# A hybrid decoder trunk on one core: the place of the down projection's weight sums, and the order of the last quarter's output

## The chip, the core and the metric

The kernel runs on 1 core of one Trainium2 chip. Time is the device time of one execution in microseconds (us), 1373.87 us as the median of three runs (1373.46 to 1376.73). The engines are named as the profile names them: PE (TensorE matmul) and PEld (its weight loads), DVE (VectorE), ACT (ScalarE), POOL (GpSimd), SP (SyncE, which issues every DMA of this kernel, one after the other). Each engine works through its own program in order; semaphores make it wait for another engine or for a DMA.

## The reference

One layer with three sub-layers on x (1024 tokens, width 1024). Each is normalised before and after, and added to the residual stream:

```python
def rmsnorm(x, g):
    xf = x * lax.rsqrt(jnp.mean(x * x, axis=-1, keepdims=True) + RMS_EPS)
    return xf * g

h = rmsnorm(x, g_mix_pre)                       # 1. token mixing
s_in, s_gate, g_u, g_vv = split(h @ w_in)
y_ssm  = gelu(s5_ssm(s_in, ...)) * sigmoid(s_gate)
y_gmlp = chunked_spatial_gate(g_u, g_vv, ...)
x = x + rmsnorm(concat([y_ssm, y_gmlp]) @ w_out, g_mix_post)
h = rmsnorm(x, g_x_pre)                         # 2. cross-attention, 4 heads, 256 memory tokens
x = x + rmsnorm(memory_cross_attention(h, rmsnorm(mem, g_mem), w_q, w_k, w_v, w_o), g_x_post)
h = rmsnorm(x, g_ffn_pre)                       # 3. gated ConvFFN, d_ff = 2816
a = causal_depthwise_conv(h @ w_up, conv_w, conv_b)
val, gate = split(a)
x = x + rmsnorm((val * gelu(gate)) @ w_down, g_ffn_post)
```

All is float32.

## The kernel before

Activations lie transposed: 128 features on the partitions, tokens along the row. The 1024 tokens are two halves of 512 (`h` = 0, 1). A float32 product is done as three matmuls on a high and a low part of both operands (`mm3`, L233): ACT writes the rounded high part, DVE or POOL subtracts it from the original and gets the low part. For streamed weights that is L131 on ACT and L134 on DVE (`Stream.split_to`), for the rest L252 and L253 (`split`). Weights are loaded by SP into four `raw` buffers (L85) and split up to six tiles ahead (`W_AHEAD`).

The work goes through the sub-layers in order: `mixers` (which ends with the K and V projections of the memory), `attention`, `ffn` (up projection and convolution), `down`. In `attention`, first both halves of the mixing's output projection run ("o1", weights w_out), then for each half the query projection, scores, softmax and weighting of four heads, and the attention's output projection ("o2"). `post` finishes a sub-layer for one half: it multiplies with the post gain and the broadcast root mean square (L723 on DVE), adds the residual (L724 on POOL), accumulates squares (L709 on ACT, L710 on POOL or DVE), and prepares the next sub-layer's input (L729, L730). It is a generator that advances by a step as matmuls are recorded (`side`, `tick`).

The statistics of a normalisation are made with PE and DVE: `rms` sums squares over partitions with matmuls against ones (L278) into a PSUM bank, and `rsqrt` finds the reciprocal root in eleven tiny DVE operations (L261 to L270). `bcast` spreads it over the partitions with matmuls against the identity (L305) and copies the result to SBUF on ACT (L308). PSUM has eight banks, tagged `acc` (4), `sx` (3) and `st` (1).

The up and down projections use Strassen's form on 2 x 2 blocks. For the down projection the sums of its weights are made early: `s_sums` loads for each of 11 row blocks four tiles of w_down (L1350, `w_dk`), makes four sums on POOL (L1354) and stores them to DRAM (L1355, `sd`). That is 44 loads, 44 sums and 44 stores. Each call of `next` makes one of 22 steps, by turns loads and sums. In the kernel before, the steps are taken in the attention's two halves: 14 steps, thus 28 sums, in the first, and the other 16 sums in the second.

`down` runs three phases of 11 blocks over four banks A and four banks B, and a fourth that completes A for the second half's tokens, first for its columns 0 to 255 (a quarter of all tokens), then for 256 to 511. Beside the fourth phase the first half's output is finished by `finish`: squares, `rms`, `bcast`, then for eight tiles the multiplication (L766, DVE), the residual (L767, POOL) and the store (L769). The second half's quarters are finished by `finish_pair` (L774 and L776, on DVE or POOL). `squares` (L1515 on ACT, L1516 on DVE) accumulates their sums of squares. `TAIL_R` and `TAIL_B` say after which (column block, row block) of the last quarter the first quarter's `rms` and `bcast` are recorded.

The order within each engine's program is set by a scheduler from the recorded order and its own estimates. Only instructions given to `pin` while `self.pinned` is set keep the order in which they are written.

## Time and profile before

| | |
|---|---|
| median of three runs | 1373.87 us (1373.46 to 1376.73) |
| profiled execution | 1375.64 us |
| its span (first to last instruction) | 1373.8 us |
| mean granted TensorE clock | 0.967 |
| PE / DVE / ACT / POOL busy | 1275.9 / 1066.1 / 628.0 / 694.6 us |
| DMA moved | 233.58 MB, 170 GB/s in the mean |

A row of the profile names a line, an engine, an operation and its tiles, output first (`m<-m,rs` writes tile m from m and rs). "Idle before" is how long the engine stood still ahead of the row, and the arrow names what ended the wait. `xN` is a count. A PE matmul of 128x512 here takes 0.23 us at the full clock; the granted clock falls to 0.5 in some stretches. SPq is SP's queue, whose rows are issues of DMAs.

### The profile page before, as it was taken

To read this page: it belongs to the slowest core of one execution; us is meant where nothing else is said; L and a number is where in the kernel's file an instruction comes from. 1 tells how busy PE (TensorE), PEld (TensorE's weight loads), DVE (VectorE), ACT (ScalarE), POOL (GpSimd) and SP (SyncE) were. 2 spreads that over 40 slices of the span, in tenths; PEclk is the share of its full clock that TensorE was granted. 3 is DMA by queue.
4 is the path that set the end of the run, shared out by engine and by line. 5 is a ranking of instruction groups with operands and counts; after the bars stand their busy time and mean duration, and the time that the engine had idled before them with its cause. 6 is when DMAs were issued, how large, how long until landed. Compare 5 with 4: busy or idle time off the path is not lost. (4 is left out here: it accounts for less than half of the span.)

```text
span 1373.8 us, 19246 instructions
## 1 busy us (share of the span) xinstructions
PE 1275.9 (93%) x6352; PEld 1080.4 (79%) x6352; DVE 1066.1 (78%) x1619; ACT 628.0 (46%) x1172; POOL 694.6 (51%) x532
## 2 busy tenths in 40 slices
PE   9799898779998999769999999999999999999993
PEld 7689897678886888558887878888888888788883
DVE  7968799876377757796657978888899879966576
ACT  7223331246444445345544654555555554446340
POOL 1586355834258524860343838656565227822144
PEclk9899999899998999979999999999999999999996
DMA  9654326256348844772358566545454359755123
GB/s 319 185 143 134 93 73 182 85 148 192 93 125 263 299 134 125 266 245 85 83 163 282 161 209 229 180 149 161 146 182 140 107 198 383 233 159 175 56 79 136
DMA packets 150662, 233.58 MB, mean 170 GB/s; under 512 B 33697, under 2 KB 43041, under 8 KB 150561
## 3 DMA queue, kind: packets, MB, share of 16 engines
q1 hardware_dynamic: 150560, 232.34, 53.3%
q8 instruction: 50, 0.82, 0.3%
q14 instruction: 52, 0.42, 0.1%
HBM read 174.23 MB, written 53.85 MB: 166 GB/s over the span
## 5 line engine op out<-in xcount | busy, mean ns | idle before, releaser
L233 PE MATMUL acc<-b,w 128*128 128x512 f32 x2412 | 587.9, 397 | 11.4 <-DVE b L730 4.4
L233 PEld LDWEIGHTS acc<-b,w 128*128 128x128 f32 x2412 | 457.6, 191 | 110.2 <-DVE b L730 6.5
L134 DVE TENSOR_TENSOR w<-raw,w 128x512 fp32r<-128x512 f32 x206 | 203.1, 994 | 94.2 <-PE acc L233 64.6
L233 PE MATMUL sx<-b,w 128*128 128x512 f32 x921 | 222.6, 391 | 1.7 <-ACT T L1277 1.7
L233 PEld LDWEIGHTS sx<-b,w 128*128 128x128 f32 x921 | 174.0, 189 | 38.5 <-ACT T L1277 2.1
L131 ACT CAST w<-raw 128x512 fp32r<-128x512 f32 x228 | 141.4, 622 | 125.3 <-PE acc L233 72.1
L710 POOL TENSOR_TENSOR ac<-ac,sq 128x512 f32<-128x512 f32 x52 | 78.3, 1513 | 153.2 <-ACT sq L709 152.6
L233 PE MATMUL acc<-T,w 128*128 128x512 f32 x528 | 127.0, 389 | 0.0
L233 PEld LDWEIGHTS acc<-T,w 128*128 128x128 f32 x528 | 99.1, 188 | 20.5
L253 DVE TENSOR_TENSOR w<-b,w 128x512 fp32r<-128x512 f32 x64 | 67.4, 1065 | 23.7 <-PE st L233 8.6
L1400 POOL TENSOR_TENSOR f<-f,f 128x512 f32<-128x512 f32 x33 | 55.0, 1678 | 48.1 <-DMA f<-fd 35.5
L1354 POOL TENSOR_TENSOR m<-m,m 128x512 f32<-128x512 f32 x44 | 62.8, 1432 | 31.3 <-DMA m<-in_w_dk 22.3
L724 POOL TENSOR_TENSOR m<-m,rs 128x512 f32<-128x512 f32 x32 | 49.3, 1545 | 48.6 <-DMA rs<-x1d 18.9
L233 PE MATMUL sx<-T,w 128*128 128x512 f32 x264 | 66.5, 389 | 0.0
L253 DVE TENSOR_TENSOR b<-f,b 128x512 fp32r<-128x512 f32 x53 | 54.4, 1041 | 4.3 <-ACT b L252 4.0
L233 PEld LDWEIGHTS sx<-T,w 128*128 128x128 f32 x264 | 49.6, 188 | 10.3
L709 ACT ACTIVATE sq<-m 128x512 f32<-128x512 f32 x66 | 41.3, 630 | 30.6 <-POOL m L724 13.5
L1216 POOL TENSOR_TENSOR b<-b,m 128x512 f32<-128x512 f32 x22 | 32.5, 1478 | 44.7 <-ACT m L1215 44.2
L115 POOL TENSOR_TENSOR st<-st,b 128x512 f32<-128x512 f32 x20 | 26.6, 1328 | 52.5 <-DMA st<-in_w_up 29.4
L252 ACT CAST w<-b 128x512 fp32r<-128x512 f32 x64 | 39.5, 619 | 27.3 <-PE acc L233 16.9
L233 PE MATMUL acc<-w,b 128*128 128x256 f32 x384 | 50.9, 290 | 0.0
L252 ACT CAST b<-f 128x512 fp32r<-128x512 f32 x53 | 32.7, 619 | 38.4 <-DVE w L253 34.3
(345 smaller groups left out, 2278.9 us busy)
## 6 DMA issues: line engine op xcount, KB each, us to landing
raw<-in_w_up SPq DMA_DIRECT2D x68, 256.0 KB, 3.0
f<-fd SPq DMA_DIRECT2D x55, 256.0 KB, 4.6
m<-in_w_dk SPq DMA_DIRECT2D x44, 256.0 KB, 4.7
sd<-m SPq DMA_DIRECT2D x44, 256.0 KB, 3.8
b<-sd SPq DMA_DIRECT2D x44, 256.0 KB, 4.0
b<-in_w_up SPq DMA_DIRECT2D x40, 256.0 KB, 2.8
raw<-in_w_out SPq DMA_DIRECT2D x32, 256.0 KB, 2.7
raw<-in_w_q SPq DMA_DIRECT2D x32, 256.0 KB, 3.4
```

Of the source, the lines that this page charges most:

```text
L115: g.tensor_tensor(p["S4"], p["12"], p["S2"], ALU.subtract)
L131: nc.scalar.copy(hi[:, :w], t[:, :w])
L134: e.tensor_tensor(lo[:, :w], t[:, :w], hi[:, :w], ALU.subtract)
L233: self.pin(nc.tensor.matmul(ps, lhsT=x, rhs=y, start=first and i + j == 0, stop=last and i == n - 1 and j == 2, skip_group_check=go_on))
L252: self.nc.scalar.copy(hi, src)
L253: (e or self.nc.vector).tensor_tensor(lo, src, hi, ALU.subtract)
L709: nc.scalar.activation(sq, src, AF.Square)
L710: (e or nc.gpsimd).tensor_tensor(acc, acc, sq, ALU.add)
L724: g.tensor_tensor(x, x, rs, ALU.add)
L1216: nc.gpsimd.tensor_tensor(val, val, gate, ALU.mult)
L1354: g.tensor_tensor(t[to], t[x], t[y], op)
L1400: self.nc.gpsimd.tensor_tensor(s[to], s[x], s[y], ALU.subtract)
```

## The change

The diff, without the parts that only move a line:

```diff
-TAIL_R = (1, 1)
-TAIL_B = (1, 9)
+TAIL_R = (0, 7)
+TAIL_B = (1, 3)
+JOB_AT = (8,)
...
-    def rms(self, acc, nt):
+    def rms(self, acc, nt, bank="st"):
...
-        ps = self.bank("st")
+        ps = self.bank(bank)
...
-    def bcast(self, r, nt, tag="st"):
+    def bcast(self, r, nt, tag="st", bank="st"):
...
-        ps = self.bank("st")
+        ps = self.bank(bank)
...
     def finish(self, m, acc, h, x2d):
...
-        r, bc = yield from self.stats(acc, 4)
+        r = self.rms(acc, 4)
+        yield
+        bc = self.bcast(r, 4)[0]
+        yield
         for i in range(KT):
             x = m[i]
-            v.scalar_tensor_tensor(x, x, self.gain["g_ffn_post"][:, i:i + 1], bc, ALU.mult, ALU.mult)
-            g.tensor_tensor(x, x, res[i], ALU.add)
+            self.pin(v.scalar_tensor_tensor(x, x, self.gain["g_ffn_post"][:, i:i + 1], bc, ALU.mult, ALU.mult))
+            e = v if i % 4 == 3 else g
+            self.pin(e.tensor_tensor(x, x, res[i], ALU.add))
+            nc.sync.dma_start(self.out[P * i:P * i + P, HALF * h:HALF * h + HALF], x)
             yield
-            nc.sync.dma_start(self.out[P * i:P * i + P, HALF * h:HALF * h + HALF], x)
...
+        s_job = self.s_sums()
         kv = self.side(kv_parts(), 1)
         for h in range(2):
             for b in range(8):
                 proj(lambda k, hh: self.mix[k, hh], "o1", m1, sq1, b, h, (4, 5, 6, 7, 0, 1, 2, 3))
+                if h == 0:
+                    next(s_job)
...
-        s_job = self.s_sums()
...
             if h == 0:
+                self.drain(s_job)
                 self.side(post[1])
...
-                    t[o, j] = self.slot("m")
+                    t[o, j] = self.slot("t" if k < 4 else "m")
...
+        next(job)
+        next(job)
         for k in range(11):
...
-            next(job, None)
-        self.drain(job)
+            if k in JOB_AT:
+                next(job)
         st = {}
+        self.pinned = True
         for b in range(4):
-            self.pinned = b > 0
             for k in range(11):
                 one(k, b, quarters[1])
+                if k % 2 == 0 and b < 2:
+                    next(job, None)
                 if (b, k) == TAIL_R:
-                    st["r"] = self.rms(sq[1][:, quarters[0]], 2)
+                    st["r"] = self.rms(sq[1][:, quarters[0]], 2, "sx")
                 if (b, k) == TAIL_B:
-                    bc = self.bcast(st["r"], 2)[1]
+                    bc = self.bcast(st["r"], 2, "st", "sx")[1]
```

Eight steps of `s_sums` (16 loads, 16 sums, 16 stores) are now taken in the first half of "o1", in tiles of the tag `t` (11 buffers), and the other 14 in the first half's attention as before; the second half's attention has none. In the tail, `finish` is advanced by a step after every second row block of the last quarter's first two column blocks, its multiplication reads the broadcast in PSUM, two of its eight additions go to DVE, and the order of all this is fixed. The first quarter's statistics come earlier and use a bank `sx`.

In the changed kernel all lines behind the edits have moved by 1 to 12: L85 is L86 there, L710 is L711, L724 is L725, L766 is L770, L767 is L772, L1350 is L1358, L1354 is L1362, L1355 is L1363 and L1516 is L1524.

SP's program where "o1" begins, in the kernel before (`raw<-in_w_v` are loads of the V projection's weights, `raw<-in_w_out` those of "o1"):

```order
L85 DMA raw_3482<-in_w_v 128x512
L85 DMA raw_3488<-in_w_v 128x512
L85 DMA raw_3519<-in_w_out 128x512
L85 DMA raw_3552<-in_w_out 128x512
L85 DMA raw_3560<-in_w_out 128x512
L85 DMA raw_3566<-in_w_out 128x512
L85 DMA raw_3597<-in_w_out 128x512
```

The same place in the changed kernel, from the fourth load of w_out on (`sd` are the stored sums):

```order
L86 DMA raw_3566<-in_w_out 128x512
L1363 DMA sd_0_229<-t_3691 128x512
L1363 DMA sd_0_251<-t_3689 128x512
L86 DMA raw_3597<-in_w_out 128x512
L1363 DMA sd_1_230<-t_3807 128x512
L1363 DMA sd_0_240<-t_3685 128x512
L86 DMA raw_3629<-in_w_out 128x512
L1363 DMA sd_1_252<-t_3805 128x512
L86 DMA raw_3653<-in_w_out 128x512
L1363 DMA sd_0_262<-t_3687 128x512
L1358 DMA t_3915<-in_w_dk 128x512
L86 DMA raw_3675<-in_w_out 128x512
```

Stores and loads of the sums now stand between the loads of w_out; ahead of these rows eleven loads of `in_w_dk` stand among the last four loads of w_v and the first three of w_out.

POOL's program in the second half's attention, in the kernel before (L710 accumulates squares, L1354 is a sum, L724 adds a residual):

```order
L710 TENSOR_TENSOR ac_5333<-ac_5333,sq_5748 128x512
L1354 TENSOR_TENSOR m_5907<-m_5907,m_5905 128x512
L1354 TENSOR_TENSOR m_6030<-m_6026,m_6030 128x512
L1354 TENSOR_TENSOR m_6026<-m_6032,m_6026 128x512
L1354 TENSOR_TENSOR m_6028<-m_6028,m_6026 128x512
L1354 TENSOR_TENSOR m_6169<-m_6167,m_6169 128x512
L1354 TENSOR_TENSOR m_6167<-m_6163,m_6167 128x512
L1354 TENSOR_TENSOR m_6163<-m_6169,m_6163 128x512
L1354 TENSOR_TENSOR m_6165<-m_6165,m_6163 128x512
L1354 TENSOR_TENSOR m_6302<-m_6300,m_6302 128x512
L724 TENSOR_TENSOR m_5331<-m_5331,rs_5933 128x512
L724 TENSOR_TENSOR m_5390<-m_5390,rs_5988 128x512
```

The same place in the changed kernel:

```order
L711 TENSOR_TENSOR ac_5397<-ac_5397,sq_5708 128x512
L711 TENSOR_TENSOR ac_5397<-ac_5397,sq_5750 128x512
L711 TENSOR_TENSOR ac_5397<-ac_5397,sq_5812 128x512
L725 TENSOR_TENSOR m_5395<-m_5395,rs_5989 128x512
L725 TENSOR_TENSOR m_5454<-m_5454,rs_6036 128x512
```

The residuals now follow the squares directly.

DVE's program in the tail, in the kernel before, from the last square of the first quarter to the first step of that quarter's reciprocal root (L281 reads the sums of squares from PSUM):

```order
L1516 TENSOR_TENSOR ac_11081<-ac_11081,sq_13145 128x256
L766 SCALAR_TENSOR_TENSOR m_12201<-m_12201,gains,st_12982 128x512
L766 SCALAR_TENSOR_TENSOR m_12206<-m_12206,gains,st_12982 128x512
L766 SCALAR_TENSOR_TENSOR m_12211<-m_12211,gains,st_12982 128x512
L766 SCALAR_TENSOR_TENSOR m_12216<-m_12216,gains,st_12982 128x512
L766 SCALAR_TENSOR_TENSOR m_12221<-m_12221,gains,st_12982 128x512
L766 SCALAR_TENSOR_TENSOR m_12226<-m_12226,gains,st_12982 128x512
L766 SCALAR_TENSOR_TENSOR m_12231<-m_12231,gains,st_12982 128x512
L766 SCALAR_TENSOR_TENSOR m_12236<-m_12236,gains,st_12982 128x512
L281 TENSOR_SCALAR st_x<-st 128x2
```

In the changed kernel, ahead of that root and then behind it (L1524 is a square of the last quarter, L772 an addition of `finish` that went to DVE, L779 and L781 are `finish_pair`):

```order
L770 SCALAR_TENSOR_TENSOR m_12201<-m_12201,gains,st 128x512
L770 SCALAR_TENSOR_TENSOR m_12206<-m_12206,gains,st 128x512
L770 SCALAR_TENSOR_TENSOR m_12211<-m_12211,gains,st 128x512
L282 TENSOR_SCALAR st_x<-sx 128x2
L262 TENSOR_SCALAR rs_y_13126<-st_x 128x2
```

```order
L770 SCALAR_TENSOR_TENSOR m_12216<-m_12216,gains,st 128x512
L772 TENSOR_TENSOR m_12216<-m_12216,rs_13004 128x512
L770 SCALAR_TENSOR_TENSOR m_12221<-m_12221,gains,st 128x512
L1524 TENSOR_TENSOR ac_11081<-ac_11081,sq_13153 128x256
L770 SCALAR_TENSOR_TENSOR m_12226<-m_12226,gains,st 128x512
L770 SCALAR_TENSOR_TENSOR m_12231<-m_12231,gains,st 128x512
L770 SCALAR_TENSOR_TENSOR m_12236<-m_12236,gains,st 128x512
L772 TENSOR_TENSOR m_12236<-m_12236,rs_13012 128x512
L779 TENSOR_TENSOR m_12287<-m_12287,st_13181 128x512
L781 TENSOR_TENSOR m_12287<-m_12287,b_12288 128x512
```

Three multiplications of the first half stand ahead of the quarter's root instead of eight, the other five behind it. On PE the first half's broadcast stands 11 matmuls behind its sums of squares (47 before), the quarter's sums 21 matmuls behind that, and its broadcast another 21 (24 before).

## Prediction

> **What bounds the kernel now.** I read the page first (engine totals, slices), then busy time by windows, then the waits and the timeline of the windows that stand out.
>
> ```profile
> PE 1275.9 (93%) x6352; PEld 1080.4 (79%) x6352; DVE 1066.1 (78%) x1619; ACT 628.0 (46%) x1172; POOL 694.6 (51%) x532
> ...
> PE   9799898779998999769999999999999999999993
> ```
>
> PE is busy 93% of the span, so it is the bound nearly everywhere, and a change can only win in the few slices below 9. Two of them are touched: slices 17 to 19 (about 550 to 620 us, digits 7, 6, 9) and the last one. The windows give the size (columns: window, length, then PE, PEld, DVE, ACT, POOL busy, granted clock, DMA share, GB/s):
>
> ```profile
> 325.00:365.00 40.00, 39.63 (x191) 33.58 (x192) 15.39 (x20) 19.43 (x36) 8.44 (x7) 1.00 0.47 136
> 428.00:510.00 82.00, 81.50 (x405) 68.81 (x406) 54.84 (x95) 35.72 (x79) 43.70 (x32) 0.95 0.74 244
> 548.00:620.00 72.00, 52.90 (x235) 40.97 (x234) 62.22 (x87) 28.02 (x59) 51.30 (x35) 0.88 0.75 251
> 1325.00:1374.00 49.00, 24.01 (x175) 23.09 (x173) 31.97 (x59) 7.10 (x19) 21.80 (x14) 0.76 0.32 108
> ```
>
> In the second half's attention (548 to 620) PE stands idle for 72.00 - 52.90 = 19.1 us; there DVE and POOL are the busy ones. The first half's (428 to 510) loses 0.5 us, though 28 of the 44 sums run in it. The stretch to which 16 sums move (325 to 365) has a full PE, a POOL that is 79% idle and a DVE that is 62% idle. In the last 49 us PE is idle for half the time.
>
> DVE and POOL slow each other, and only for some operands:
>
> ```profile
> L766 DVE SCALAR_TENSOR_TENSOR m<-m,gains,st x8: 746/1745/1785, 1333.3 to 1343.0; 128x512 f32<-128x512 f32 x8
> L1205 DVE SCALAR_TENSOR_TENSOR t<-acc,conv,t x6: 731/739/750, 770.6 to 824.5; 128x511 f32<-128x511 f32 x6
> 770.00:780.00 10.00, 10.00 (x46) 8.29 (x45) 9.96 (x10) 4.48 (x10) 10.00 (x8) 1.00 0.78 234
> ```
>
> (A line's durations are minimum, median, maximum in ns.) With both tensors in SBUF the operation takes 0.75 us in a gap of POOL and 1.75 us beside it. The same operation with one tensor in PSUM takes 0.73 to 0.75 us, although POOL is busy all of 770 to 780.
>
> **Part 1: sixteen sums leave the second half's attention.** What they take there, and what waits:
>
> ```profile
> PE acc L233 <- DVE b L730: 4.4, 3, 2.4
> ...
> L1354 POOL TENSOR_TENSOR m<-m,m 128x512 f32<-128x512 f32 x16 | 23.6, 1477 | 10.4 <-DMA m<-in_w_dk 9.2 <-DMA rs<-x1d 0.5 <-issue 0.2
> L269 DVE SCALAR_TENSOR_TENSOR rs_t<-rs_t,st_x 128x4 f32<-128x4 f32 x6 | 4.0, 663 | 0.2
> L723 DVE SCALAR_TENSOR_TENSOR m<-m,gains,st 128x512 f32<-128x512 f32 x8 | 9.5, 1259 | 0.0
> ...
> 569.27 1.28 POOL L1354 TENSOR_TENSOR m<-m,m 128x512 f32<-128x512 f32 x1
> 574.13 1.07 DVE L261 TENSOR_SCALAR rs_y<-st_x 128x4 int32<-128x4 int32 x1
> 582.09 0.17 DVE L739 TENSOR_SCALAR rs_y<-rs_y 128x4 f32<-128x4 f32 x1
> 583.14 0.56 ACT L1128 ACTIVATE t<-sx,mx,rs_y 128x256 f32<-128x256 f32 x1 [10.65 <-DVE mx L1124]
> 585.97 1.11 PE L233 MATMUL sx<-kv,t 128*128 128x256 f32 x4 [3.47 <-ACT t L252]
> 587.73 3.31 PE L233 MATMUL acc<-b,w 128*128 128x512 f32 x10
> 598.52 5.74 PE L233 MATMUL acc<-b,w 128*128 128x512 f32 x24
> 611.40 1.12 PE L1142 MATMUL sx<-ident,t 128*128 128x128 f32 x4 [7.15 <-ACT t L1128]
> 615.88 6.99 PE L233 MATMUL acc<-b,w 128*128 128x512 f32 x21
> ...
> 610.00:620.00 10.00, 7.26 (x19) 5.51 (x20) 8.75 (x16) 6.57 (x17) 4.02 (x3) 0.50 0.71 225
> ```
>
> The tiny steps of the reciprocal root average 0.66 us here and 0.16 us elsewhere (last fence, below); the whole root takes from 574.1 to 582.3. It holds the first maxima, so the exponentials wait 10.65 us, and PE 3.47 us for the ACT copy behind them. Then eight L723 in a row (9.5 us) stand ahead of the next maxima, and PE waits 7.15 us. After it PE runs at a granted clock of 0.50: 21 matmuls take 6.99 us where 24 take 5.74, which loses 2.0 us; the 10 at 587.73 lose 0.9 us in the same way.
>
> Without the sums, POOL has nothing left between its last squares and the first L724, so the root falls from some 8 us to some 2 (eleven steps of 0.16 and their gaps) and the 3.47 us goes: **-3.5**. The L723 go from 9.5 to 8 x 0.75 = 6.0 plus about 1 each beside two L724, and the three operations ahead of the maxima lose about 1: the stall falls from 7.15 to about 3, **-4.1**. Of the 19.1 us idle, 10.6 is named so far; 4.4 is PE's wait for L730, ahead of the half's first sum at 569.27, and stays; of the other 4.1 I take half, **-2.0**. The halved clock cost 2.9 and should mostly go with the long stalls: **-2.4**. Together **-12**. The bounds: -4 (the first stall and its clock alone) and -20 (all but the 4.4, the clock, and 2 to 3 for loads that land sooner). What is late next is DVE's own row of L723 and the adds of the same sub-layer, which is why 3 us of the second stall stay.
>
> **Part 2: they arrive in the first half's output projection.** The loads there, PE's last wait before it, PE's pace, the splits of 330 to 390, and the landing of the stores that go along:
>
> ```profile
> 321.94 67.19 SPq L85 DMA_DIRECT2D raw<-in_w_out  x31
> 325.37 4.45 PE L233 MATMUL acc<-w,m 128*128 128x256 f32 x35 [0.71 <-DVE w L134]
> 803.98 5.44 PE sx L233 x24
> L134 DVE TENSOR_TENSOR w<-raw,w 128x512 fp32r<-128x512 f32 x24 | 20.1, 845 | 34.9 <-PE acc L233 33.7 <-ACT w L131 1.1
> DMA to landing us min/median/max: 2.0/3.9/6.8
> ```
>
> POOL gets 16 x 1.3 to 1.48 = 21 to 24 us on top of 8.4 of 40: it fits. DVE's splits (L134, 0.845 us mean) may go to 1.75, sixteen of them 14 us more, on 15.4 of 40: it fits. On SP the 16 stores stand between the 4th and the 18th load of weights, each waiting for its sum. Each load feeds 12 matmuls, 5.44 / 2 = 2.72 us; those 14 feed PE for 38 us. The sums with the two K/V splits and two accumulations that stand among them take POOL about 29 us, and the last five loads wait for slots whose stores land in 3.9 us, perhaps two of them one after the other: 37 us, with some six splits in stock. So PE should not wait in the middle. At the start, where PE waited 0.71 us for a split, eleven loads are put among the last of w_v and the first of w_out: I take **+1**, from nothing to +4. These are covered by POOL's and DVE's idle time; if that cover fails, see the third rival.
>
> **Part 3: the last quarter.**
>
> ```profile
> 1325.09 0.95 PE L278 MATMUL st<-ones,ac 128*128 128x1 f32 x8
> 1328.91 0.16 DVE L270 SCALAR_TENSOR_TENSOR rs_y<-rs_t,rs_y 128x4 f32<-128x4 f32 x1
> 1333.33 11.47 DVE L766 SCALAR_TENSOR_TENSOR m<-m,gains,st 128x512 f32<-128x512 f32 x8 [1.38 <-ACT st L308]
> 1344.72 0.15 DVE L281 TENSOR_SCALAR st_x<-st 128x2 f32<-128x2 f32 x1
> 1348.55 0.16 DVE L270 SCALAR_TENSOR_TENSOR rs_y<-rs_t,rs_y 128x2 f32<-128x2 f32 x1
> 1348.86 1.19 PE L305 MATMUL st<-ident,rs_y 128*128 128x128 f32 x4 [11.94 <-DVE rs_y L270]
> 1350.49 3.91 PE L233 MATMUL acc<-f,w 128*128 128x256 f32 x18
> 1356.03 2.32 PE L233 MATMUL acc<-f,w 128*128 128x256 f32 x18
> 1360.61 0.43 DVE L1516 TENSOR_TENSOR ac<-ac,sq 128x256 f32<-128x256 f32 x1 [2.37 <-ACT sq L1515]
> ...
> L774 DVE TENSOR_TENSOR m<-m,st x5: 678/686/1774, 1352.0 to 1367.1; 128x512 f32<-128x512 f32 x5
> L774 POOL TENSOR_TENSOR m<-m,st x3: 1270/1272/1734, 1350.5 to 1365.3; 128x512 f32<-128x512 f32 x3
> L269 DVE SCALAR_TENSOR_TENSOR rs_t<-rs_t,st_x 128x4 f32<-128x4 f32 x3 | 0.5, 160 | 0.1
> ```
>
> Today eight L766 stand ahead of the quarter's reciprocal root, PE waits 11.94 us, and its next 18 matmuls take 3.91 us instead of 2.32. Now only three stand ahead of it. PE's side: 11.94 + 1.6 = 13.5 us go. New waits come. The first broadcast stands 11 matmuls (1.4 us at 2.32 / 18) behind the sums of squares instead of 47, while the root is ready 3.0 us after them: PE waits 1.6 us. The quarter's broadcast waits for its own root, 4.0 us beside POOL's adds (1344.7 to 1348.7 today), of which 21 matmuls hide 2.7: 1.3, with the trip to DVE and back about 2. PE is done 9.9 us sooner.
>
> DVE's and POOL's side ends later. From 1326.0 on: root 3.0, broadcast 1.1, 21 matmuls 2.7, sums of squares 0.6, the quarter's root 4.0: 1337.4. Behind it come five multiplies at 0.75 us, which read PSUM and pass POOL by, and seven POOL operations of 1.28 us, six DVE operations of 0.68 and three squares of 0.43 that take turns: 9.0 + 4.1 + 1.3 = 14.4 us, and about 1.5 us in which POOL waits for the multiplies. The last square is added by 1353.7, not by 1361.0, and what follows (12.8 us to the end) stays: **-7.3**. Bounds: -3, if the root takes 8 us as at 574 and the multiplies 1.75, and -9.9, PE's side alone. The ACT copy of the broadcast stays in the program and the first multiply still waits for it, so nothing is counted for it.
>
> [...]
>
> **The sum** is +1 - 12 - 7.3 = **-18.3 us**. The profiled execution took 1375.64 us (its span of 1373.8 and 1.8 around it) and would take 1357.3. The median of the runs is 1373.87, 1.8 below it, so I forecast **1355.6 us**.
>
> **The rivals.**
> - *The sums did not hold the second half; its own post-processing does.* For it: 428 to 510 carries 28 sums and PE loses 0.5 us. Against it: there the first half's post-processing was over before them, and steps of 0.66 us are seen only beside a busy POOL. Part 1 would bring -5: 1 - 5 - 7.3 gives 1362.6. Chance 0.17.
> - *The tail only changes its bound.* First half and quarter now share DVE and POOL; if the root is slowed to 8 us, part 3 is -3: 1359.9. Chance 0.13. [...]
> - *The stores hold SP (slower).* If each of the 16 stores in the output projection costs SP a sum and a landing, 1.48 + 3.9 = 5.4 us, SP needs 86 us for loads that feed 38, with 16 (six splits) in stock: PE loses 32 us, and -19.3 + 32 gives 1386.6. It decides the sign from 73 us, 4.6 per store. Against it: a store does not wait for the one before it, and 28 sums go with their stores through 428 to 510. Chance 0.05.
> - *POOL held all of it*: part 1 is -20, 1347.6. Chance 0.10.
> - *The change does not do what it says*: other waits take both gains back, 1373. Chance 0.04.
>
> **How the numbers follow.** The forecast (1350 to 1359) keeps 0.51. The range, 1347 to 1365, takes in the first, second and fourth rival and their bounds and leaves out about 2 in 10: the fifth and third rival (0.09) and the far ends of the others. About 0.3%, 4.1 us, is what a measurement can tell from no change: faster 0.91, within it 0.04, slower 0.05.
>
> **What would show it.** Part 1: between 548 and 620 of the old scale PE idle falls from 19 to 8 or 9 us, L269 there is near 0.16 us, and the clock stays at 1.00. Wrong if the waits for L1128 keep their 7 us. Part 2: PE stays above 39 of 40 us in the output projection; wrong if PE waits for L134 or SP's loads of w_out stretch. Part 3: no wait of PE above 4 us after the sums of squares, L770 at 0.75 us, and 1325 to the end shorter by 7. What would make the forecast wrong is above all a new wait of PE in the first half, which no row of this profile shows.

## The result, and the profile after the change

| | before | after |
|---|---|---|
| median of the runs compared | 1375.23 us (1373.46 to 1376.73) | 1351.42 us (1349.37 to 1352.44) |
| profiled execution | 1375.64 us | 1352.44 us |
| its span | 1373.8 us | 1350.6 us |
| mean granted clock in it | 0.967 | 0.972 |

The ratio is 0.9825 with a 95% interval from 0.9806 to 0.9845, so the change saves 23.8 us (21.3 to 26.7). The forecast was 18.3 us less, 1355.6 us, with a range from 1347 to 1365.

The totals of the page and PE's slices, in the changed kernel. The 7, 6, 9 of slices 17 to 19 have become 8, 8, 9, and the last slice has gone from 3 to 5:

```profile
PE 1270.8 (94%) x6352; PEld 1077.3 (80%) x6352; DVE 1060.4 (79%) x1621; ACT 628.2 (47%) x1172; POOL 698.0 (52%) x530
...
PE   9799898779997999889999999999999999899995
```

The windows that the prediction looked at, in the changed kernel (window, length, PE, PEld, DVE, ACT and POOL busy, granted clock, DMA share, GB/s). The last one begins with the first half's sums of squares, which stood at 1325.09 before:

```profile
325.00:365.00 40.00, 37.76 (x182) 31.48 (x183) 26.25 (x19) 19.01 (x34) 35.60 (x23) 1.00 0.91 317
428.00:510.00 82.00, 78.26 (x398) 66.44 (x399) 54.39 (x95) 36.79 (x82) 47.32 (x34) 0.96 0.73 248
548.00:620.00 72.00, 63.24 (x311) 51.11 (x309) 59.48 (x104) 35.05 (x75) 30.68 (x21) 0.95 0.53 159
1310.29:1350.50 40.21, 24.80 (x174) 24.10 (x172) 27.19 (x61) 7.10 (x19) 17.33 (x12) 0.75 0.38 131
```

Between 548 and 620 PE now stands idle for 72.00 - 63.24 = 8.8 us, where it was 19.1; POOL's time there has fallen from 51.3 to 30.7 us. (The work that ended near 620 now ends near 608; the 12 us behind that have no idle time. The 3.7 us lost in the second row are the wait of 6.5 us ahead of the attention, which stood before 428 in the old profile and reaches behind it now.) Between 325 and 365 POOL has gone from 8.4 to 35.6 us, and PE's idle time from 0.4 to 2.2 us.

For all that follows the span is cut into stages at places that every kernel has on PE: the first matmul of the last part of the mixing (M, near 295), and the rows of L278 (L279 after), which sum squares: of the first half's o1 (A, near 382), of the residual behind it (B, 430), of the second half's o1 (C, 520), of its residual (D, 568), of the first half's o2 residual (E, 631 before, 619 after), and of the first half's output (T). Lengths in us, worked out from the starts of these rows in each kernel's timeline; the last row is the time of the profiled execution:

| stage | before | after | sums alone | tail alone | copy read | adds left out | tiles of m | PSUM in post | best | before, PSUM in post |
|---|---|---|---|---|---|---|---|---|---|---|
| to M | 294.8 | 295.6 | 295.4 | 293.6 | 296.9 | 295.5 | 295.2 | 292.5 | 294.8 | 293.9 |
| M to A | 85.8 | 88.5 | 86.6 | 86.7 | 88.3 | 86.5 | 93.1 | 86.3 | 87.9 | 85.6 |
| A to B | 47.6 | 47.6 | 46.4 | 46.7 | 47.1 | 46.8 | 49.5 | 43.7 | 45.0 | 43.8 |
| B to C | 92.0 | 90.3 | 90.4 | 92.1 | 91.7 | 92.2 | 89.4 | 91.9 | 90.2 | 92.6 |
| C to D | 47.9 | 46.2 | 46.3 | 48.5 | 46.4 | 48.3 | 46.3 | 43.1 | 43.3 | 45.9 |
| D to E | 63.3 | 51.2 | 51.1 | 62.0 | 51.0 | 47.2 | 51.3 | 46.8 | 46.9 | 58.5 |
| E to T | 693.7 | 690.9 | 693.5 | 693.0 | 693.5 | 696.5 | 695.2 | 690.0 | 690.9 | 690.4 |
| T to end | 48.7 | 40.3 | 48.0 | 39.3 | 42.8 | 48.2 | 40.1 | 39.2 | 38.4 | 48.3 |
| profiled run | 1375.6 | 1352.4 | 1359.2 | 1363.5 | 1359.4 | 1362.9 | 1362.1 | 1335.3 | 1339.1 | 1360.7 |

The places to look at are M to A (the sums arrive), D to E (they have left) and T to the end. In E to T and in the stretch to M these kernels hardly differ, and yet they are 3 to 6 us apart from execution to execution; a whole time stands in that noise, a stage much less. (The profiled execution of "PSUM in post" is the fastest of its four, by 5.7 us.) The columns are named as the experiments below.

### The profile page after: what moved, and what is told of

Its sections match the earlier page's. It is cut to its first block, busy times and chain, and to the rows that moved or that the text cites. A ratio compares the mean times of both kernels' runs of the same rounds, so it can differ in the third digit from the quotient of the medians.

```text
span 1350.6 us, 19229 instructions
## 1 busy us (share of the span) xinstructions
PE 1270.8 (94%) x6352; PEld 1077.3 (80%) x6352; DVE 1060.4 (79%) x1621; ACT 628.2 (47%) x1172; POOL 698.0 (52%) x530
## 4 chain that ended last, share of the span: by engine, by line
PE 63%; DVE 16%; DMA 9%; issue 4%; POOL 4%; ACT 2%; SPq 1%; DVEq 0%; POOLq 0%; ACTq 0%
PE acc L234 42%; PE sx L234 17%; DVE w L135 3%; PE st L234 2%; DMA rs<-in_xT 1%; POOL ac L711 1%; DVE w L254 1%; DVE m L724 1%; POOL m L725 1%; PE st L306 1%; DMA m<-in_xT 1%; DVE b L254 1%; DMA b<-in_w_dk 1%; DMA b<-sd 1%; DMA x<-x 1%
## 5 line engine op out<-in xcount | busy, mean ns | idle before, releaser
L135 DVE TENSOR_TENSOR w<-raw,w 128x512 fp32r<-128x512 f32 x206 | 211.5, 1036 | 85.9 <-PE acc L234 43.8
L711 POOL TENSOR_TENSOR ac<-ac,sq 128x512 f32<-128x512 f32 x52 | 80.0, 1546 | 142.5 <-ACT sq L710 99.1
L725 POOL TENSOR_TENSOR m<-m,rs 128x512 f32<-128x512 f32 x32 | 49.5, 1552 | 63.2 <-DVE m L724 30.8
L1408 POOL TENSOR_TENSOR f<-f,f 128x512 f32<-128x512 f32 x33 | 56.1, 1712 | 47.2 <-DMA f<-fd 28.8
L234 PEld LDWEIGHTS sx<-T,w 128*128 128x128 f32 x264 | 49.5, 188 | 10.3
L710 ACT ACTIVATE sq<-m 128x512 f32<-128x512 f32 x66 | 41.3, 630 | 32.3 <-POOL m L725 12.9
L253 ACT CAST b<-f 128x512 fp32r<-128x512 f32 x53 | 32.7, 619 | 40.1 <-DVE w L254 35.4
L135 POOL TENSOR_TENSOR w<-raw,w 128x512 fp32r<-128x512 f32 x22 | 29.9, 1363 | 37.8 <-ACT w L132 23.5
```

Of the source, the lines that this page charges most:

```text
L135: e.tensor_tensor(lo[:, :w], t[:, :w], hi[:, :w], ALU.subtract)
L234: self.pin(nc.tensor.matmul(ps, lhsT=x, rhs=y, start=first and i + j == 0, stop=last and i == n - 1 and j == 2, skip_group_check=go_on))
L253: self.nc.scalar.copy(hi, src)
L710: nc.scalar.activation(sq, src, AF.Square)
L711: (e or nc.gpsimd).tensor_tensor(acc, acc, sq, ALU.add)
L725: g.tensor_tensor(x, x, rs, ALU.add)
```

## The experiments

**The two halves apart.** The first two runs take the change apart: the move of the sums without the new tail, and the new tail without the move. Together their diffs are that of the change.

> The kernel before with the move of the 16 sums alone; the tail is that of before. Theory (the sums held DVE and POOL in the second half's attention): the stages before the tail end as in the changed kernel, so this gives the changed kernel's gain without the tail's 8.4 us: 1375.2 - 23.8 + 8.4 = 1360 us, and from 1325 on PE waits 11.9 us for the last quarter's root as before. Rival (half of the gain before the tail is chance in the granted clock, which shows -1.7, -2.1 and -0.5 us in stages that the change does not touch): 1364 to 1366 us. Rival (moving the sums gains nothing and the tail did it all): 1372 us or more.

> The kernel before with the new tail alone; the sums stay in the second half. Theory: the last stage, from the first half's sums of squares to the end, is 40.3 us long as in the changed kernel instead of 48.6, and nothing else moves: 1375.2 - 8.4 = 1366.8 us, and the two parts add up to the whole. Rival (the parts depend on each other, for instance by the state of the clock at the tail): 1370 us or more, with half clock for more than the first 10 us of the stage.

Measured: the sums alone 1359.86 us (ratio 0.9909, 0.9892 to 0.9925; 13.8 us less than 1373.66 in the same comparison), the tail alone 1367.05 us (0.9955, 0.9936 to 0.9974; 6.6 us). Both are where the theory had them, and they add up to 20.4 us. In the table the sums alone have D to E at 51.1 and the old tail; the tail alone has the old 62.0 and the new tail at 39.3.

**The mechanism of the second half.** In the kernel before, the arithmetic of the last 16 sums is left out, while their loads and stores stay:

```diff
             def put(n, to, x, y, op=ALU.subtract):
-                g.tensor_tensor(t[to], t[x], t[y], op)
+                if k < 7:
+                    g.tensor_tensor(t[to], t[x], t[y], op)
                 nc.sync.dma_start(self.sd[n][k], t[to])
```

> The kernel before without the arithmetic of the last 16 sums: their loads and stores stay where they are, and the stored tiles are the loaded ones, so this part of the down projection's weights isn't the sums. Theory (POOL's 16 operations themselves slow DVE): the reciprocal roots take about 2 us, the waits of 3.5 us and 7.1 us go or fall below 2, and the stretch from the second half's sums of squares (568) to the first half's next sums of squares (631) shrinks from 63.3 to about 51 us: 1375.2 - 12 = 1363 us. Rival (the loads, stores and buffers of tag m are what holds the second half): it stays at 60 to 63 us, 1373 us or more.

Measured 1363.39 us (0.9931, 0.9909 to 0.9953), with D to E at 47.2 us. So it was POOL's arithmetic, not the traffic: with the loads and the stores in place the stage is even 4 us shorter than in the changed kernel. The timelines of DVE and PE show where the 4 us are. First the changed kernel, from the root to the end of what it delays:

```profile
573.78 0.17 DVE L262 TENSOR_SCALAR rs_y<-st_x 128x4 int32<-128x4 int32 x1
576.26 0.17 DVE L740 TENSOR_SCALAR rs_y<-rs_y 128x4 f32<-128x4 f32 x1
578.52 0.56 ACT L1136 ACTIVATE t<-sx,mx,rs_y 128x256 f32<-128x256 f32 x1 [5.55 <-DVE rs_t L264]
585.64 9.58 DVE L724 SCALAR_TENSOR_TENSOR m<-m,gains,st 128x512 f32<-128x512 f32 x8 [1.10 <-ACT st L309]
600.11 0.66 PE L1150 MATMUL sx<-ident,t 128*128 128x128 f32 x4 [1.74 <-ACT t L1136]
601.68 0.51 PE L234 MATMUL sx<-kv,t 128*128 128x256 f32 x2 [0.91 <-ACT t L253]
603.61 0.52 PE L234 MATMUL sx<-kv,t 128*128 128x256 f32 x1 [1.43 <-DVE t L254]
604.79 6.52 PE L234 MATMUL acc<-b,w 128*128 128x512 f32 x23
```

Then the same in the kernel without the adds:

```profile
585.98 7.46 DVE L723 SCALAR_TENSOR_TENSOR m<-m,gains,st 128x512 f32<-128x512 f32 x8 [1.10 <-ACT st L308]
599.42 0.66 PE L1142 MATMUL sx<-ident,t 128*128 128x128 f32 x4 [0.71 <-ACT t L1128]
603.09 5.17 PE L233 MATMUL acc<-b,w 128*128 128x512 f32 x22
```

In both the root takes 2.6 us and the wait of 3.47 us is gone. What is left is the row of eight multiplications (9.58 and 7.46 us), the waits behind it, and in the changed kernel 23 matmuls that run in part at the half clock (6.52 us where 22 take 5.17; the granted clock over these 6.5 us is 0.82). The multiplications are long because POOL's additions of the residual (L725) run beside them: four in the changed kernel, two where the loads of the residuals come later behind those of the sums (POOL waits 5.46 us for the third there, 1.66 in the changed kernel).

**The operand.** If that is so, the multiplication should not suffer when it reads the broadcast in its PSUM bank. Three runs ask that at three places. In the changed tail, `finish` goes back to the copy in SBUF:

```diff
-        bc = self.bcast(r, 4)[0]
+        bc = self.bcast(r, 4)[1]
```

> The changed kernel, but finish multiplies with the copy of the broadcast in SBUF instead of reading the bank; the order is the same on every engine. Theory (an operation of DVE with both tensors in SBUF takes turns with POOL, one with a tensor in PSUM does not): the multiplies beside a POOL addition go from 0.74 to about 1.75 us, five or six of the eight, +5 us on DVE's chain, of which the first three (+2) delay the quarter's root: the tail is 4 to 5 us longer, 1356 us. [...]

Measured 1359.11 us (0.9889, 0.986 to 0.9919), but the runs went from 1351.46 to 1359.41, and 4.6 of the 7.0 us between the two profiled executions lie ahead of T, where the edit changes nothing. The tail itself is 42.8 us long, 2.5 more. Line L770 in this kernel (minimum, median and maximum in ns):

```profile
L770 DVE SCALAR_TENSOR_TENSOR m<-m,gains,st x8: 736/748/1780, 1321.7 to 1333.5; 128x512 f32<-128x512 f32 x8
```

Its first three and its last three in DVE's timeline:

```profile
1321.69 3.11 DVE L770 SCALAR_TENSOR_TENSOR m<-m,gains,st 128x512 f32<-128x512 f32 x3 [2.85 <-ACT st L309]
1331.09 4.14 DVE L770 SCALAR_TENSOR_TENSOR m<-m,gains,st 128x512 f32<-128x512 f32 x3
```

In the changed kernel the same two groups take 2.06 and 2.05 us. So the mechanism is the one expected, and the price of 4 to 5 us was too high: three multiplications are slowed, not five or six, since others fall into gaps of POOL.

The other way round, the old tail in the old order with the bank read in place of the copy (and the bank sx for the quarter's statistics, as the bank is now held longer):

```diff
-        r, bc = yield from self.stats(acc, 4)
+        r = self.rms(acc, 4)
+        yield
+        yield
+        bc = self.bcast(r, 4)[0]
```

> The kernel before, its tail in the old order, but finish multiplies with the broadcast in its PSUM bank; the quarter's statistics take the bank sx for that. Theory (operand and order each give a part of the tail's 8.4 us; with the copy in the new order the stage was 42.8 us long): the eight L766 take 6.0 instead of 11.5 us, PE's wait for the quarter's root falls from 11.9 to about 6.5, and the stage from the first half's sums of squares to the end is 43 to 44 us long instead of 48.7: 1368 us. Rival (the order alone matters): 48 us, 1373 us, because the additions on POOL and the last products wait as before. Rival (the operand alone matters): 40 us, 1365 us.

Measured 1369.74 us (0.9958, 0.994 to 0.9975); the tail is 44.7 us long. The eight multiplications in DVE's timeline, and the wait for the quarter's root behind them in PE's:

```profile
1331.55 5.36 DVE L769 SCALAR_TENSOR_TENSOR m<-m,gains,st 128x512 f32<-128x512 f32 x8
...
1343.08 1.22 PE L305 MATMUL sx<-ident,rs_y 128*128 128x128 f32 x4 [8.87 <-DVE rs_y L270]
```

Old tail with the copy 48.3 us (mean of the four kernels of the table that have it), operand alone 44.7, order alone 42.8, both 39.7 (mean of four). So the operand alone brings 3.6 us and the order alone 5.5, each in one profiled execution, and both together 8.6. The multiplications fall by 6.1 us (11.47 to 5.36), the wait only by 3.1: the tiny operations of the root, which now stand beside POOL's additions, are still slowed by them (of the nine behind the multiplications five take 0.56 to 1.22 us and four 0.16; the nine take 6.2 us, where the whole root took 4.0).

The third place is `post`, in the attention, in the changed kernel with everything else as it is:

```diff
-        r, bc = yield from self.stats(acc, 4)
+        r = self.rms(acc, 4)
+        yield
+        yield
+        bc = self.bcast(r, 4)[0]
         yield
         acc2 = self.slot("ac")
```

> The changed kernel, but post's multiplication with the post gain reads the broadcast in its PSUM bank instead of the copy in SBUF; the order is the same on every engine. Theory (with both tensors in SBUF the multiplication takes turns with POOL's additions, with one in PSUM it does not): the eight L724 ahead of the second half's second maxima take 6.0 us instead of 9.6, PE's waits of 1.7, 0.9 and 1.4 us behind them go and with them 1.0 us of half clock: the stretch from the second half's sums of squares to the next (568 to 619) shrinks from 51.2 to about 47.5, as in the run without the adds (47.2); with nothing to 1 us in each of the two post-processings before, 1347 us. Rival (what is left there is ACT's and the loads' doing): 1351 us, with L724 at 6.0 us all the same. [...]

Measured 1342.46 us (0.9788, 0.9761 to 0.9816), more than was expected. The groups of this line over the whole span, first in the changed kernel, then in this one (busy time, mean ns):

```profile
L724 DVE SCALAR_TENSOR_TENSOR m<-m,gains,st 128x512 f32<-128x512 f32 x32 | 38.3, 1264 | 5.6 <-ACT st L309 5.6
```

```profile
L727 DVE SCALAR_TENSOR_TENSOR m<-m,gains,st 128x512 f32<-128x512 f32 x32 | 21.5, 742 | 5.6 <-ACT st L309 5.6
```

The same 32 operations in the same places take 742 ns instead of 1264. The table shows it in all the post-processings: A to B 3.9 us less, C to D 3.1, D to E 4.4. (The fourth post-processing is in E to T.)

**Which of the two, the place or the operand?** The kernel before with this edit alone, the sums still in the second half:

> The kernel before, with post's multiplication reading PSUM and nothing else; the order is the same on every engine. Theory (the operand gains what it gained in the changed kernel in the post-processings that the sums do not touch, 3.5, 3.1 and 2.1 us, and the second half's long wait of 7.1 us falls to about 3.5, while the slow reciprocal root and its 3.5 us stay): 1373.7 - 12 = 1361 to 1362 us, and the stretch from the second half's sums of squares to the next, 63.3 us, shrinks to about 59 us. Rival (with the multiplications out of POOL's way the sums do no harm in the second half): 47 to 51 us, 1353 us, and the move of the sums would have been unnecessary.

Measured 1360.67 us (0.9897, 0.9879 to 0.9915), D to E 58.5 us. The timelines of PE and of DVE, with PE's waits, the first and last step of the root, and the eight multiplications:

```profile
579.61 0.73 PE L233 MATMUL sx<-kv,t 128*128 128x256 f32 x4 [3.47 <-ACT t L252]
600.78 1.08 PE L1145 MATMUL sx<-ident,t 128*128 128x128 f32 x4 [2.71 <-ACT t L1131]
...
567.77 1.07 DVE L261 TENSOR_SCALAR rs_y<-st_x 128x4 int32<-128x4 int32 x1
575.73 0.17 DVE L742 TENSOR_SCALAR rs_y<-rs_y 128x4 f32<-128x4 f32 x1
587.96 5.35 DVE L726 SCALAR_TENSOR_TENSOR m<-m,gains,st 128x512 f32<-128x512 f32 x8
```

The row of multiplications is down to 5.35 us and the long wait from 7.15 to 2.71, but the root still takes 8 us (567.77 to 575.73) and its wait of 3.47 us is untouched. So the move of the sums was needed for the root, and the operand for the multiplications: two stalls with one cause, POOL's arithmetic (without it the root takes 2.6 us and the long wait is 0.71).

**The price at the new place.** The moved sums have M to A at 86.3 to 88.5 us; to see whether it is their start beside the splits of K and V that costs this, they get tiles of tag m, by which the scheduler spreads them, two between any two squares:

```diff
-                    t[o, j] = self.slot("t" if k < 4 else "m")
+                    t[o, j] = self.slot("m")
```

> The changed kernel, but the moved sums use tiles of tag m like the others; by that the scheduler puts them later, two of them between any two squares of the first half's o1, and none among the splits of K and V. Theory (what the moved sums cost there comes from their first six, which run beside the K/V splits while PE has no split weights in stock): the stretch from the last mixing matmul (295) to the first half's sums of squares (382) takes 86.3 us as in the kernels without moved sums, not 86.6 to 88.5, and the time is 1 to 2 us shorter, 1350 us. Rival (the cost comes from the sums as such, wherever in o1 they run): 1351.4 us. Rival (the four tiles of m per block come too late and the sums hold the next stage): 1354 us or more.

Measured 1360.51 us (0.991, 0.9884 to 0.9937), 9 us above the changed kernel. M to A is 93.1 us (0.7 us of it are three matmuls that stand behind A in the other kernels), so the theory fell, and the third case holds, by a way that it had not named. ACT, which makes the first part of the split weights, waits for their loads, POOL for those of the sums, and SP's next loads of w_out stand behind stores that wait for the sums (timelines of ACT, POOL, SP and PE):

```profile
384.12 0.62 ACT L132 CAST w<-raw 128x512 fp32r<-128x512 f32 x1 [6.27 <-DMA raw<-in_w_out]
...
383.47 3.12 POOL L1362 TENSOR_TENSOR m<-m,m 128x512 f32<-128x512 f32 x2 [4.20 <-DMA m<-in_w_dk]
...
379.10 1.60 SPq L86 DMA_DIRECT2D raw<-in_w_out  x3
384.76 2.18 SPq L1363 DMA_DIRECT2D sd<-m  x2
...
388.31 1.86 PE L279 MATMUL st<-ones,ac 128*128 128x1 f32 x8 [5.44 <-POOL ac L711]
```

Between 380.7 and 384.8 SP issues nothing: the store at its head waits for a sum that waits for its load. The last square stands on POOL behind two such sums, and PE waits 5.44 us for it. This is the rival of the prediction in which the stores hold SP, and with the tiles of t it stays away: eleven free tiles let eleven loads go out ahead of the first store, and SP stands still at a store for 2.1 us at most. The run changes the order of the sums together with their tiles, so it does not separate the two.

**What the first quarter's products wait for.** In the changed kernel, the two products that DVE makes for the first quarter of the second half read the bank as well:

```diff
-                    bc = self.bcast(st["r"], 2, "st", "sx")[1]
+                    ps1, bc = self.bcast(st["r"], 2, "st", "sx")
...
-                    st["out"] = self.chain(*(self.finish_pair(mg[0][i], res[0][i], wide(bc), i, 1, 0, v)
+                    st["out"] = self.chain(*(self.finish_pair(mg[0][i], res[0][i], wide(ps1), i, 1, 0, v)
```

> The changed kernel, but the two products that DVE makes for the first quarter of the second half (L779) read the broadcast in its PSUM bank; the order is the same on every engine. Theory (turns with POOL): the two go from 1.77 to about 0.7 us, the last squares come 1.5 to 2 us sooner, PE's wait of 3.3 us for them falls below 2: 1349.8 us. Rival (POOL's own ten operations are what the last squares wait for, since L781 behind the products takes its turn all the same): no change, 1351.4 us.

Measured 1352.18 us (0.9854, 0.983 to 0.9879): no difference that the times can tell. The trace has the products at 0.68 us and PE's wait for the last square at 2.0 instead of 3.3 us, as the theory said, and the tail at 38.3 us (1352.9 - 1314.6), 1.4 less than the mean above. But the last two squares take 2.91 us instead of 0.94 (DVE's timeline):

```profile
1337.63 2.91 DVE L1524 TENSOR_TENSOR ac<-ac,sq 128x256 f32<-128x256 f32 x2
```

That they now come together with POOL's last operations is an estimate from that length: in the changed kernel such a square takes 1.51 us beside POOL's L781 and 0.42 where POOL is idle.

**All edits together, and the best of them.** With the reads in PSUM in both multiplications of `post` and in the quarter, and the tiles of m:

> The changed kernel with the last three edits together, and post's second multiplication (the pre gain of the next sub-layer) reading its broadcast in PSUM as well. Theory: the parts add up, 1351.4 - 1.4 - 4.5 - 1.6 = 1344 us, and up to 1 us less for the second multiplication, whose bank nobody else needs at that time. Rival (they share one slack, or the bank st, held longer, stops PE): 1348 us or more, with PE waiting for a bank.

Measured 1344.99 us (0.9798, 0.9775 to 0.982), on the theory's number for the wrong reason: it has the loss of the m tiles in it (M to A 93.0 us) and the larger gain of `post`. Without the m tiles, and without the second multiplication, whose 16 operations get shorter (744 ns instead of 939) while the stage around them keeps its length:

> The changed kernel with post's multiplication and the first quarter's two DVE products reading PSUM; the sums stay in tiles of t. Theory: what the run with all edits lost against the one with post alone (93.0 and 47.5 us where that has 86.3 and 43.7, in the first half's o1 and behind it) came from the tiles of m, so this is at the run with post alone or 1 us below it, 1341.5 to 1342.5 us. Rival (the reads of PSUM hold the bank and cost time elsewhere): 1345 us or more.

Measured 1338.18 us (0.9731, 0.971 to 0.9752), 36.3 us less than before and faster than the changed kernel, whose interval begins at 0.9806. That is 3 to 4 us less than the theory; of the stages that the two edits touch only the tail is shorter than with PSUM in `post` alone (38.4 against 39.2 us), so where the rest comes from stays open.

**Is it any operation of POOL?** In a single execution, `finish` reads the copy, and POOL's additions are replaced by a multiplication of one tensor with a constant:

```diff
-        bc = self.bcast(r, 4)[0]
+        bc = self.bcast(r, 4)[1]
...
-            self.pin(e.tensor_tensor(x, x, res[i], ALU.add))
+            self.pin(e.tensor_tensor(x, x, res[i], ALU.add) if e is v else g.tensor_scalar(x, x, 2.0, None, ALU.mult))
```

> The changed kernel with the multiplication of finish reading the copy in SBUF, and with POOL's six additions of the residual left out: POOL multiplies the tile by a constant instead, so the first half's output is not the reference's. One look, for the durations. Theory (any operation of POOL takes turns with an operation of DVE whose tensors are both in SBUF): multiplications beside POOL take longer than 0.75 us by about the POOL operation's time, as in the run with the copy (3.1 us for the first three, 4.1 us for the last three). Rival (only a POOL operation with two tensors does): 2.06 us for three, as with the bank.

The two lines in this run (durations as above):

```profile
L770 DVE SCALAR_TENSOR_TENSOR m<-m,gains,st x8: 739/749/1098, 1319.8 to 1329.0; 128x512 f32<-128x512 f32 x8
L772 POOL TENSOR_SCALAR m<-m x6: 1484/1654/1927, 1320.7 to 1330.4; 128x512 f32<-128x512 f32 x6
```

The same two groups of three in DVE's timeline:

```profile
1319.83 2.43 DVE L770 SCALAR_TENSOR_TENSOR m<-m,gains,st 128x512 f32<-128x512 f32 x3 [1.93 <-ACT st L309]
1327.35 2.77 DVE L770 SCALAR_TENSOR_TENSOR m<-m,gains,st 128x512 f32<-128x512 f32 x3
```

Neither case: three take 2.43 and 2.77 us, against 3.11 and 4.14 beside POOL's additions and 2.06 from PSUM. The longest is 0.35 us above 0.75, not a whole operation of POOL. In one execution that is all that can be said.

## Why the prediction was right

**Part 1, the sums leave (forecast -12).** D to E fell from 62.9 (mean of before, the tail alone, and the old tail with the bank) to 51.1 us (mean of after, the sums alone, the copy): -11.8. PE's idle time between 548 and 620 of the old scale was forecast at 8 or 9 us and is 8.8. In the profiled pair PE's idle time from D to E fell by 9.2 us (13.6 to 4.4), where the forecast had 3.5 + 4.1 + 2.0 = 9.6, and its busy time by 2.9 (49.6 to 46.7), where it had 2.4 for the clock. The root went from 8 us to 2.6, as its rows say (mean ns of the tiny step, in the kernel before 663):

```profile
L270 DVE SCALAR_TENSOR_TENSOR rs_t<-rs_t,st_x 128x4 f32<-128x4 f32 x6 | 0.9, 158 | 0.1
```

and the wait of 3.47 us is gone. One step inside was wrong: "The L723 go from 9.5 to 8 x 0.75 = 6.0 plus about 1 each beside two L724". They take 9.58 us. The step counted the additions that ran beside them before; with POOL free and the loads earlier, four come instead of two. That the wait behind the row fell all the same, from 7.15 to 1.74 us and so further than to the forecast's 3, is in part luck. From the first maximum behind the row to the last (L1123 to L1124, now L1131 to L1132) DVE takes 3.1 us where it took 5.9, and the forecast had taken off about 1; and the row begins 1.7 us behind the start of PE's broadcast where it was 3.1. Two short waits that follow, 0.45 and 0.88 us before, are 0.91 and 1.43 now, and a piece of half clock is left where "the clock stays at 1.00" had been said (it is 0.95 over the window). What hangs on the multiplications is shown by the run with PSUM in `post`: D to E is 46.8 us, the 23 matmuls that take 6.52 us in the changed kernel take 5.38, and of the three waits one is left, 1.78 us.

**Outside that stage** the prediction counted nothing. C to D is 1.9 us shorter in the mean where the sums have moved (46.2 to 46.4 against 47.9 to 48.5). Most of that is the border between the stages and not a gain. PE's last row ahead of D, in the kernel before and in the changed one:

```profile
556.72 10.48 PE L233 MATMUL acc<-b,w 128*128 128x512 f32 x44 [1.71 <-DVE b L730]
559.47 8.90 PE L234 MATMUL acc<-b,w 128*128 128x512 f32 x38 [0.45 <-DVE b L731]
```

Six matmuls of 0.23 us, 1.4 us in all, now stand behind D. For equal work D to E fell by 13.2 us and C to D by 0.5; the sum of the two is the same. So the closeness of -11.8 to the forecast's -12 owes something to where the border fell. (The kernel without the adds has the 38 as well. Its C to D of 48.3 us has a slower clock in it, 0.93 in the mean against 0.96 in the changed kernel: these 38 take 11.00 us there.)

**Part 2, the sums arrive (forecast +1, from 0 to +4).** M to A is 87.5 us in the mean of the changed kernel, the sums alone, the copy, PSUM in `post` and the best, and 86.1 in the mean of the four without moved sums: +1.4. Single executions of the two groups overlap (86.3 to 88.5 and 85.6 to 86.7). The place is the one that was named, the start. PE's waits there, and a wait of ACT, which makes the first part of these splits:

```profile
315.01 10.94 PE L234 MATMUL acc<-w,m 128*128 128x256 f32 x84 [0.77 <-DVE w L135]
326.65 1.09 PE L234 MATMUL acc<-w,m 128*128 128x256 f32 x7 [0.71 <-DVE w L135]
328.35 3.62 PE L234 MATMUL acc<-w,m 128*128 128x256 f32 x28 [0.60 <-DVE w L135]
333.37 50.84 PE L234 MATMUL acc<-b,w 128*128 128x512 f32 x223 [0.93 <-DVE w L135]
...
329.02 0.62 ACT L132 CAST w<-raw 128x512 fp32r<-128x512 f32 x1 [2.37 <-DMA raw<-in_w_out]
```

PE's waits come to 3.0 us where the old kernel has 1.2 at this place. They are waits for L135, which the prediction had named (as L134) among the signs of being wrong; the splits are late because ACT waits for loads of w_out, between which SP issues the loads for the sums. From 333.4 on, 223 matmuls run without a gap beside the other ten sums, as forecast. That PE would stay above 39 of 40 us was too much: it is 37.8.

**Part 3, the tail (forecast -7.3, from -3 to -9.9).** It fell from 48.3 to 39.7 us in the means: -8.6. The steps in the timeline of the changed kernel:

```profile
1310.29 0.95 PE L279 MATMUL st<-ones,ac 128*128 128x1 f32 x8
1314.41 2.05 PE L306 MATMUL st<-ident,rs_y 128*128 128x128 f32 x8 [1.76 <-DVE rs_y L271]
1321.37 0.34 DVE L262 TENSOR_SCALAR rs_y<-st_x 128x2 int32<-128x2 int32 x1
1323.31 0.16 DVE L271 SCALAR_TENSOR_TENSOR rs_y<-rs_t,rs_y 128x2 f32<-128x2 f32 x1
1336.92 0.94 DVE L1524 TENSOR_TENSOR ac<-ac,sq 128x256 f32<-128x256 f32 x2
1338.01 0.98 PE L279 MATMUL st<-ones,ac 128*128 128x1 f32 x4 [3.34 <-DVE ac L1524]
```

In the tail alone PE also waits for the quarter's root, which it does not in the changed kernel:

```profile
1334.64 0.71 PE L306 MATMUL sx<-ident,rs_y 128*128 128x128 f32 x4 [1.44 <-DVE rs_y L271]
```

The line of the multiplications in the changed kernel:

```profile
L770 DVE SCALAR_TENSOR_TENSOR m<-m,gains,st x8: 735/738/748, 1317.1 to 1327.1; 128x512 f32<-128x512 f32 x8
```

PE's first new wait is 1.76 us (1.6 forecast), no wait is above 3.34 us (4), the multiplications take 738 ns (0.75), and the last square is added 27.6 us behind the first half's sums of squares (forecast: 1353.7 - 1325.1 = 28.6). The quarter's root, put at 4.0 us, takes 4.0 in the tail alone, and PE's second wait is 1.44 us there (2 forecast). In the changed kernel it takes 2.3 us and PE does not wait, but nothing is won by that: behind its first wait PE runs at the half clock (0.50 from 1314.3 to 1320.3), so the root begins 2.7 us later, when POOL's first three additions are nearly over, and it ends 13.2 us behind T, against 12.1 in the tail alone and 12.3 in the forecast. What was mis-sized is the stretch from there to the last square: 14.4 us in both executions, where the terms come to 14.4 + 1.5 = 15.9 (and the time written down, 1353.7, holds 0.4 more than their sum). So the 1.5 us in which POOL was to wait for the multiplications did not come. That DVE and POOL, not PE, end the tail is as forecast: PE waits 3.34 us for the last square.

A multiplication that reads the bank takes no longer here than one that reads the copy in a gap of POOL: 735 to 748 ns, 738 in the median, with the bank, and 736 at the least and 748 in the median with the copy.

**The rivals.** That the second half's own post-processing held it (0.17; part 1 at -5) fell, with a grain of truth in it: with the sums gone its multiplications still cost 4.4 us, which PSUM in `post` brought back. That the tail only changes its bound (0.13) did not come either: no root there takes 8 us. The half clock did come there, behind the first wait of 1.76 us (granted clock 0.50 in the changed kernel). The stores that hold SP (0.05) were seen with the m tiles, at 7 us in the stage and 2 to 3 behind it instead of 32. That POOL held all of it (0.10) fell short.

**The sum.** The parts, measured in stages, give -11.8 - 1.9 + 1.4 - 8.6 = -20.9, and the two halves apart gave 20.4 us. The measured 23.8 has some 3 us more. Part of that lies in the kernel before: its median is 1375.23 us in this comparison and 1373.66, 1371.69 and 1374.52 in the three later ones. In the profiled pair E to T is 2.8 us shorter and B to C 1.7, stages that vary as much between kernels that hardly differ there; that the rest is chance is argued from that and not shown by a run.

## What to carry to other kernels

Look at the spread of one line's durations before its mean: here two values, 746 ns at the least and 1745 in the median for the multiplications of the tail, led to the turns that the line takes with POOL, and one operand in PSUM (742 ns instead of 1264 in `post`), or POOL's work put elsewhere (the root in 2.6 us instead of 8), took the turns away. When work is moved on SP's queue, ask whether its loads have buffers to run ahead; the same sums in the same stage cost 1.4 us with free tiles and some 6 without (with another order as well). And when a stall is priced, ask what its freed engine will do sooner: the additions that came forward, four instead of two, took back what the multiplications had been given (9.58 us for the row, 9.54 before).

## What the runs showed of the hardware

**Turns between DVE and POOL.** Beside an operation of POOL with two tensors in SBUF, DVE operations with both tensors in SBUF took up to some 1 us longer, the small ones too. In the second half's attention of the kernel before, the root's steps take 0.16 us or 1.07 to 1.21; the steps at 574.13 and 575.24 end at 575.20 and 576.45, and the POOL operations that had begun before them, at 573.70 and 575.14, end at 575.18 and 576.43. So these steps look as if they waited for the operation of POOL to end. The multiplications of the run with the copy, 748 ns in the median and 1780 at the most beside additions of 1287 to 1735, agree with that. In the single execution with one-tensor operations on POOL no multiplication takes more than 1.10 us beside POOL operations of 1.65 us in the median, which does not look like a wait for a whole operation. With one operand in PSUM the 32 multiplications of `post` take 736 to 748 ns, with both in SBUF 736 to 1835.

**The half clock behind a gap of 1.76 us.** The changed kernel runs at half clock after a gap of 1.76 us in the tail, and the tail alone, with the same tail and the same gap, does not. Two windows of each, from 2 us and from 4 us behind the first half's sums of squares, first the changed kernel:

```profile
1312.29:1314.29 2.00, 0.36 (x4) 0.16 (x2) 1.83 (x10) 1.41 (x5) 0.00 (x0) 0.85 0.00 0
1314.29:1316.29 2.00, 1.88 (x9) 1.91 (x10) 0.00 (x0) 0.00 (x0) 0.00 (x0) 0.50 0.03 8
```

```profile
1324.48:1326.48 2.00, 0.37 (x4) 0.16 (x2) 1.84 (x10) 1.42 (x5) 0.00 (x0) 1.00 0.00 0
1326.48:1328.48 2.00, 1.88 (x16) 1.91 (x17) 0.09 (x1) 0.59 (x1) 0.00 (x0) 1.00 0.03 8
```

The granted clock is the column before the last two, and the count of matmuls in the second window (9 and 16) says the same. So behind the same gap the clock fell in one execution and not in the other. The same gap of 1.76 us stands in all nine profiled executions with the new order in the tail: behind it the eight matmuls of the broadcast (L306) take 1.88 to 2.05 us in six and 1.13 us in three (the tail alone, PSUM in `post`, and the one-tensor operations on POOL). The lowest granted clock of a 2 us window there is 0.50 to 0.57 in four of the six (the changed kernel, the copy, the quarter's products, the best) and 1.00 in the tail alone and with PSUM in `post`. The tails that are otherwise the same are 40.3 and 40.1 us long with the half clock (changed kernel, tiles of m) and 39.3 and 39.2 without. What decides between the two is not shown.
